# The output projection of a hybrid encoder block as seven half-size products, in two passes over K

## The chip, the cores and the metric

One core of a Trainium2 chip runs the whole block. The metric is device time in microseconds of one execution, as the median of several runs; a profiled execution gives the trace. All matrices are float32. TensorE (PE) is fed float32r: every float32 matrix is split into a high and a low part, and a product is the sum of three matmuls (high x high, high x low, low x high).

## The reference, cut to what matters

```python
h = rmsnorm(x, norm_w)                                  # x: (1, 1024, 2048)
proj = einsum('bsd,de->bse', h, w_in)                   # w_in: (2048, 5632)
q_a, k_a, v_a, g_a, q_r, k_r, v_r, g_r = split(proj)    # 1024,256,256,1024 | 512,512,1024,1024
attn = windowed_attention(q_a, k_a, v_a, sink, rel_bias)          # 16 heads of 64, +-128 tokens
attn = rmsnorm(attn, attn_out_norm_w) * silu(g_a)                 # 1024 wide
ret = bidirectional_retention(rotary(q_r), rotary(k_r), v_r, decays)   # 8 heads, chunks of 128
ret = head_groupnorm(ret, ret_gn_w) * silu(g_r)                   # 1024 wide
mixed = concatenate([attn, ret], axis=-1)                         # (1, 1024, 2048)
x = x + einsum('bse,ed->bsd', mixed, w_out)                       # w_out: (2048, 2048)
return rmsnorm(x, final_norm_w)
```

## The kernel before, in words

The work has three passes of PE, with the smaller engines' work laid beside them.

1. **Input units, first kind** (`STD`, lines 1224 to 1290): six units of 256 columns over the full K of 2048, 16 K-tiles each (keys, values and queries of attention).
2. **Input units, second kind** (`FAST`, 16 units of 256 columns: the gates `ga` and `gr`, the retention's `qk` and `vr`). Each is computed in two halves of K. The first 1024 of K go as **seven products of half size** (Strassen's scheme; `slots`, `prep`, `multiply`, `collect`, lines 1063 to 1168): the weight tiles of a unit are added and subtracted on GpSimd (POOL, `prep_sums`), each of the seven results is split (ACT high part, POOL low part, line 161 under `split`), and multiplied with one of seven sets of four rows `hT`, combined beforehand from the normalised input by `combine`. A product is 4 K-tiles x 3 = 12 matmuls of 128 x 128 by 512 columns. Attention runs beside this pass. The partial results go to DRAM (`yd`). The second 1024 of K go as plain products in a second loop over the 16 units (line 1370 on), which adds `yd` back; retention runs beside it.
3. **Output projection** (line 1427 on): for each half of the tokens and each of four blocks of 512 output columns, 16 K-tiles; the mixed branches are the stationary side, `w_out` the moving side (lines 1456 to 1458). The 112 weight tiles that are streamed are each split by ACT and DVE into rings of three (`w_split`, `w_load`); 16 more are split by ACT and POOL into `hT` for the last column block (lines 1478 to 1480), which runs token block by token block so that each block can be normalised and stored early (`finish_out`, `finish_last`).

Between 2 and 3 lies `mixer` (`mixed_pair`, lines 940 to 977): it loads the gate (`gd`), attention's inverse norm (`rbd`) and the branch output (`md`), multiplies them on POOL, and writes the split result into `hT`. Before it, `gate_post` applies SiLU and stores the gates to `gd`.

**What sets the order.** `point()` is called after every three 512-column matmuls (0.68 us). It lets queues of generators advance: `jobs` (attention, retention; one step every `pace` points), `aux` and `post`, and it sends stores off some points after their data was made. So the program's order is written out by hand; below that, the framework's scheduler may still reorder each engine's instructions by priority when their inputs are expected. `SP` issues nearly all DMAs, in one line; a load that waits for its buffer holds what stands behind it. PSUM has two banks `Ma`, two `Mb`, three `ST`, one `O`. At the third unit of the second loop (u = 2) the kernel drains what is left of attention and its norm, and opens the retention's buffers.

Of the kernel before, what the change touches and what calls it, by code (L numbers as in the profile page):

```python
# [28 lines left out]
FAST = [("ga", 0), ("qk", 0), ("vr", 0), ("gr", 0), ("qk", 1), ("vr", 1), ("gr", 1), ("ga", 1)]  # L29
FAST += [("qk", 2), ("vr", 2), ("gr", 2), ("qk", 3), ("vr", 3), ("gr", 3), ("ga", 2), ("ga", 3)]  # L30

ROWS = [0, 1, 8, 9, 2, 3, 10, 11, 12, 13, 4, 5, 14, 15, 6, 7]
# [6 lines left out]
def hybrid_block(ctx: ExitStack, tc: tile.TileContext, a: dict, out: bass.AP):  # L39
    nc = tc.nc  # L40
    V, A, G, T, SP = nc.vector, nc.scalar, nc.gpsimd, nc.tensor, nc.sync
# [15 lines left out]
    yd = dram.tile([NF, 4, 128, 512], F32, name="yd")  # L57
    rqk = dram.tile([4, 2, 128, S], F32, name="rqk")
# [9 lines left out]


    hT = hp.tile([128, 28, 1024], F32R, name="hT")  # L70
# [10 lines left out]

    cnt = [0]
    phase = [stp]

    def nm(p):
        cnt[0] += 1
        return f"{p}{cnt[0]}"
# [26 lines left out]

    def held(t, bufs):
        tag, n = serial[t.name]

        return t
# [82 lines left out]
    def w_src(i):  # L201
        if i >= W_ALL:
            i -= W_ALL
            return a["w_out"][(16 * (i // 16) + ROWS[i % 16] if i < 64 else i) % 64]
        if i >= W_STD:
            return a["w_half"][i - W_STD]
        u, j = divmod(i, 8)
        return a["w_in"][8 * u + (j + 7) % 8 if u == NS - 1 else i]

    def w_load(i):  # L210
        if i < n_w[0] and i not in wraw and i not in wsp:
            if i < W_STD:
                r = et_("e11")
            elif i < W_ALL:
                r = rt(F32)
            else:
                r = et_(("e11", "e2", "e12", "e2", "e11", "e12", "e2")[(i - W_ALL) % 7])
            SP.dma_start(r, w_src(i))
            wraw[i] = r

    def w_split(i):
        if i < n_w[0] and i not in wsp:
            hi, lo = wpair(i)
            split(hi, lo, wraw.pop(i), G if i < W_ALL else V)
            wsp[i] = (hi, lo)
# [23 lines left out]
    rowq, rdue = deque(), [0]  # L249
    pt, due, pace, adue, apace = [0], [0], [3.0], [0], [2.0]  # L250

    def point():
# [6 lines left out]
        if rowq and pt[0] >= rdue[0]:  # L259
            rdue[0] = max(rdue[0], pt[0] - 1) + 2.4  # L260
            pump(rowq, 1)
# [3 lines left out]

    def rows_in():
        order = list(range(20)) + list(range(24, 28)) + list(range(20, 24))
        lo = None
        for n in range(len(order) + 3):
            if n < len(order):  # L270
                c_load(0, order[n])
            if n >= 3:
                r = order[n - 3]
                first = 16 * (NS - 1) + r // 2 + 3
                if step[0] < first:
                    yield lambda: step[0] >= first
                lo = c_split(r)
                yield
                lo()
                done.add(("row", r))  # L280
            else:
                yield
# [28 lines left out]
    def hx(k, part, c0, c1):  # L311
        if k < 14:
            return hT[:, 2 * k + part, c0:c1]
# [215 lines left out]
    def q_post(i, tiles):  # L529
        for b, t in enumerate(tiles):  # L530
            et, hf = b // 2, b % 2
            for part in range(2):
                x = t2(F32R)
                if part == 0:
                    A.copy(x, t)
                    hi = x
                else:
                    tt(V, x, t, hi.bitcast(F32), ALU.subtract)
                last = (lambda: done.add(("qa", i))) if b == 3 and part else None
                store(qsd[2 * i + et, part, :, 512 * hf : 512 * hf + 512], x.bitcast(F32), x, last, 10)  # L540
            yield
# [163 lines left out]


    fetched = {}

    def ret_job(p):
# [21 lines left out]
        if "vt" not in fetched.get(p, {}):  # L731
            fetch(p, "rk")
            fetch(p, "vt")
            for _ in range(4):
# [48 lines left out]
        def scan(ah, h, q):  # L783
# [15 lines left out]
            if h == 1:  # L799
                gb = cdec[64:128, 8 + 2 * p + ah : 9 + 2 * p + ah]  # L800
                for n in range(5, -1, -1):
                    stt(V, s[64:128, 128 * n : 128 * n + 128], s[64:128, 128 * n + 128 : 128 * n + 256], gb,
                        s[64:128, 128 * n : 128 * n + 128], ALU.mult, ALU.add)
# [24 lines left out]
        def spread(ah, h, on):  # L828
            if True:
# [9 lines left out]
                tt(G, y, v, mhalf[:, :4], ALU.pow)  # L839
                O[ah, h] = (on, mv2, v, y)  # L840

# [18 lines left out]
        def o_tr(ah, h):  # L860
# [14 lines left out]
        for todo in (  # L875
# [40 lines left out]
            for f in held_back:  # L916
                f()
# [10 lines left out]
    omix = {}  # L928

    def orow(kk, hf, part):  # L930
        sl = slice(512 * part, 512 * part + 512)
        if hf == 0:
            n = ROWS.index(kk)
            return hT[:, 16 + n if n < 12 else n - 12, sl]
        return hT[:, 4 + kk, sl] if kk < 12 else omix[kk][part]

    def mixed_pair(pair, hf):

        sl = slice(512 * hf, 512 * hf + 512)
        G_, N_, R_ = {}, {}, {}  # L940

        def loads(kk):
            ring = t2 if kk >= 8 else lambda: rt(F32)
            if kk < 8:
                G_[kk], N_[kk] = ring(), ring()
                SP.dma_start(G_[kk], gd[128 * kk : 128 * kk + 128, sl])
                SP.dma_start(N_[kk], rbd[:, sl])
            R_[kk] = ring()
            SP.dma_start(R_[kk], md[128 * kk : 128 * kk + 128, sl])

        def gates(kk):
            tt(G, G_[kk], G_[kk], N_[kk], ALU.mult)
            tt(G, R_[kk], R_[kk], G_[kk], ALU.mult)

        def high(kk):
            if hf and kk >= 12:
                omix[kk] = (rt(F32R), rt(F32R))
            A.activation(orow(kk, hf, 0), R_[kk], AF.Copy, scale=ew[:, kk : kk + 1])

        def low(kk):  # L960
            stt(V, orow(kk, hf, 1), R_[kk], ew[:, kk : kk + 1], orow(kk, hf, 0).bitcast(F32), ALU.mult, ALU.subtract)
            done.add(("mix", kk, hf))

        plan = []
        for n, kk in enumerate(pair):
            at = 5 * n
            plan.append((at, n, loads, kk))
            if kk < 8:
                at += LAGS[hf][0]
                plan.append((at, n, gates, kk))  # L970
            at += LAGS[hf][1] if kk < 8 else LAGS[hf][0] - 2
            plan.append((at, n, high, kk))
            at += LAGS[hf][2]
            plan.append((at, n, low, kk))
        t0 = pt[0]
        for at, _, f, kk in sorted(plan, key=lambda x: x[:2]):
            yield lambda: pt[0] >= t0 + at
            f(kk)
        yield
# [26 lines left out]
    staged = {}  # L1006

    def c_load(ph, r):
        staged[r] = t2()
        SP.dma_start(staged[r], xd[r] if ph else cd[r])  # L1010

    def c_split(r):
        x = held(staged.pop(r), NT2)
        hi = hT[:, r, 0:512]
        A.copy(hi, x)
        return lambda: tt(V, hT[:, r, 512:1024], x, hi.bitcast(F32), ALU.subtract)

    SP.dma_start(nw, a["nw"])
# [43 lines left out]

    def raw_room(q, which):
        if q < NF:
# [583 lines left out]
```

## Time and profile before

| | us |
|---|---|
| median of 3 runs | 1549.68 (1547.74 to 1553.69) |
| profiled execution, its own time | 1547.16 |
| its span, first to last instruction | 1545.4 |

| stretch of the span | us | what runs |
|---|---|---|
| 0 to 296.0 | 296 | six full units, normalisation of the input |
| 296.0 to 734.0 | 438 | first K half of 16 units, with attention |
| 734.0 to 1177.3 | 443 | second K half of 16 units, with retention |
| 1177.3 to 1535.8 | 358 | output projection |
| 1535.8 to 1545.4 | 10 | after the last matmul |

The profile is read from three sides: how long each engine is busy in a stretch (a busy PE is not PE at its pace, since a matmul's recorded time of 389 ns covers more than the distance to the next one), what an engine waited for, and the order of single instructions.

### The profile page before, as it was taken

To read this page: it belongs to the slowest core of one execution; us is meant where nothing else is said; L and a number is where in the kernel's file an instruction comes from. 1 tells how busy PE (TensorE), PEld (TensorE's weight loads), DVE (VectorE), ACT (ScalarE), POOL (GpSimd) and SP (SyncE) were. 2 spreads that over 40 slices of the span, in tenths; PEclk is the share of its full clock that TensorE was granted. 3 is DMA by queue.
4 is the path that set the end of the run, shared out by engine and by line. 5 is a ranking of instruction groups with operands and counts; after the bars stand their busy time and mean duration, and the time that the engine had idled before them with its cause. 6 is when DMAs were issued, how large, how long until landed. Compare 5 with 4: busy or idle time off the path is not lost.

```text
span 1545.4 us, 21741 instructions
## 1 busy us (share of the span) xinstructions
PE 1503.5 (97%) x7442; PEld 1258.8 (81%) x7442; DVE 787.5 (51%) x1732; ACT 633.2 (41%) x1341; POOL 552.6 (36%) x433
## 2 busy tenths in 40 slices
PE   8999999899999999999999999999999999999997
PEld 6998887777888888887878888788888788887886
DVE  5563335764564664665043735747364433464323
ACT  5311134665775775775212232232324333434210
POOL 3232221347556557546251533525233410113000
PEclk9999999999999999999999999999999999999999
DMA  8889568586456456446566463564636855575403
GB/s 305 294 261 325 187 185 278 183 267 186 135 152 190 126 156 210 149 126 225 174 204 212 163 224 127 181 218 132 232 114 213 277 159 153 179 238 186 124 19 109
DMA packets 185034, 292.83 MB, mean 189 GB/s; under 512 B 28203, under 2 KB 66091, under 8 KB 184284
## 3 DMA queue, kind: packets, MB, share of 16 engines
q1 hardware_dynamic: 152156, 266.28, 53.6%
q10 hardware_dynamic: 32768, 25.17, 5.0%
q8 instruction: 58, 0.95, 0.3%
q14 instruction: 52, 0.43, 0.1%
HBM read 204.84 MB, written 86.54 MB: 189 GB/s over the span
## 4 chain that ended last, share of the span: by engine, by line
PE 76%; DMA 9%; DVE 6%; issue 3%; ACT 3%; POOL 2%; SPq 1%; ACTq 0%; POOLq 0%; DVEq 0%
PE psMa L1403 3%; PE psMb L1403 3%; PE psMa L1405 3%; PE psMa L1404 3%; PE psMb L1404 3%; PE psMb L1405 3%; PE psMa L1100 3%; PE psMa L1101 3%; PE psMa L1102 3%; PE psMb L1100 2%; PE psMb L1102 2%; PE psMb L1101 2%; PE psST L1457 2%; PE psST L1458 2%; PE psST L1456 2%
## 5 line engine op out<-in xcount | busy, mean ns | idle before, releaser
L161 POOL TENSOR_TENSOR wl<-r,wh 128x512 fp32r<-128x512 f32 x176 | 233.0, 1327 | 400.4 <-ACT wh L167 376.0
L167 ACT CAST wh<-e 128x512 fp32r<-128x512 f32 x160 | 97.9, 618 | 213.7 <-PE psMb L1458 63.1
L167 ACT CAST wh<-r 128x512 fp32r<-128x512 f32 x176 | 108.3, 617 | 156.3 <-PE psMb L1404 75.4
L161 DVE TENSOR_TENSOR wl<-e,wh 128x512 fp32r<-128x512 f32 x112 | 88.3, 797 | 133.6 <-ACT wh L167 133.0
L161 POOL TENSOR_TENSOR r<-r,r 128x512 f32<-128x512 f32 x96 | 131.1, 1374 | 53.1 <-DMA r<-rbd 46.3
L161 POOL TENSOR_TENSOR wl<-e,wh 128x512 fp32r<-128x512 f32 x48 | 70.4, 1470 | 198.1 <-ACT wh L167 166.4
L1403 PE MATMUL psMb<-hT,wh 128*128 128x512 f32 x256 | 105.7, 413 | 1.5 <-DVE e L161 1.5
L1100 PE MATMUL psMa<-hT,wh 128*128 128x512 f32 x256 | 102.6, 401 | 2.9 <-DVE e L161 2.9
L1403 PE MATMUL psMa<-hT,wh 128*128 128x512 f32 x256 | 104.0, 406 | 0.3 <-ACT on L853 0.3
L1101 PE MATMUL psMa<-hT,wh 128*128 128x512 f32 x256 | 101.3, 396 | 0.0
L1102 PE MATMUL psMa<-hT,wl 128*128 128x512 f32 x256 | 101.3, 396 | 0.0
L1405 PE MATMUL psMb<-hT,wl 128*128 128x512 f32 x256 | 100.3, 392 | 0.0
L1404 PE MATMUL psMb<-hT,wh 128*128 128x512 f32 x256 | 100.2, 392 | 0.0
L1405 PE MATMUL psMa<-hT,wl 128*128 128x512 f32 x256 | 100.0, 391 | 0.0
L1404 PE MATMUL psMa<-hT,wh 128*128 128x512 f32 x256 | 99.8, 390 | 0.0
L648 DVE CUSTOM_DVE_ANT_0 P<-psST,bias,nsink 128x384 f32<-128x384 f32 (+1 forms) x128 | 74.3, 580 | 33.3 <-PE psST L640 31.8
L652 ACT ACTIVATE P<-P,nmx 128x385 f32<-128x385 f32 (+1 forms) x128 | 75.9, 593 | 34.9 <-DVE nmx L648 33.2
L1100 PE MATMUL psMb<-hT,wh 128*128 128x512 f32 x192 | 75.7, 394 | 0.0
L1102 PE MATMUL psMb<-hT,wl 128*128 128x512 f32 x192 | 75.2, 392 | 0.0
L1101 PE MATMUL psMb<-hT,wh 128*128 128x512 f32 x192 | 75.1, 391 | 0.0
L161 DVE TENSOR_TENSOR PTl<-psST,PTh 128x384 fp32r<-128x384 f32 (+1 forms) x128 | 66.5, 520 | 16.0 <-ACT PTh L629 15.6
L161 POOL TENSOR_TENSOR hT<-t,hT 128x512 fp32r<-128x512 f32 x16 | 21.6, 1351 | 122.1 <-ACT hT L167 122.0
(350 smaller groups left out, 3928.4 us busy)
## 6 DMA issues: line engine op xcount, KB each, us to landing
e<-in_w_out SPq DMA_DIRECT2D x112, 256.0 KB, 3.1
r<-in_w_fast SPq DMA_DIRECT2D x64, 256.0 KB, 3.2
r<-in_w_half SPq DMA_DIRECT2D x64, 256.0 KB, 3.7
e<-yd SPq DMA_DIRECT2D x64, 256.0 KB, 4.0
t<-in_xT SPq DMA_DIRECT2D x31, 512.0 KB, 6.0
e<-in_w_in SPq DMA_DIRECT2D x48, 256.0 KB, 4.8
yd<-e SPq DMA_DIRECT2D x48, 256.0 KB, 3.1
t<-in_x SPq DMA_DIRECT2D x16, 512.0 KB, 5.8
```

Of the source, the lines that this page charges most:

```text
L161: eng.tensor_tensor(o, x, y, op)
L167: A.copy(o_hi, x)
L648: V.tensor_tensor_reduce(x[:, :W], p[:, :W], bias[2 * pr + c][:, k0 : k0 + W], -1.0, nsink[:, head : head + 1], ALU.add, ALU.min, nmx[:, c ...
L652: A.activation(x[:, : W + 1], x[:, : W + 1], AF.Exp, bias=nmx[:, c : c + 1], scale=-1.0, accum_out=sums[:, c : c + 1])
L1100: T.matmul(bank, wh[:, ws], hh, start=(j == 0 and p in (0, 1, 3)), stop=False, skip_group_check=True)
L1101: T.matmul(bank, wh[:, ws], hl, start=False, stop=False, skip_group_check=True)
L1102: T.matmul(bank, wl[:, ws], hh, start=False, stop=(j == 3), skip_group_check=True)
L1403: T.matmul(p, wh[:, ws], hh, start=(w, kk) == (0, 0), stop=False)
L1404: T.matmul(p, wh[:, ws], hl, start=False, stop=False)
L1405: T.matmul(p, wl[:, ws], hh, start=False, stop=last)
L1456: T.matmul(p, mh, wh, start=(k == 0), stop=False)
L1457: T.matmul(p, mh, wl, start=False, stop=False)
```

## The change

What it does, part by part:

- The output projection becomes 16 units. A unit is 256 tokens x 1024 output columns x 1024 of K, done as seven products of 128 x 512 x 512 by the helpers of the input units. Now the mixed branches take the place of the weights (token tiles `xm`, combined on POOL unit by unit), and the combinations of `w_out` take the place of the rows.
- The order is four stages `st = 2 * (half of K) + (half of the columns)` of four units each. Half 0 of K holds attention's first 512 features and retention's first two groups, half 1 the rest. Stages 0 and 1 store partial sums (with x added) to `yo`; stages 2 and 3 add them back and finish.
- The weight combinations (28 rows for each stage) are made once and kept in DRAM (`wc`): `w_copies` copies the 12 that need no arithmetic, DRAM to DRAM, beside attention; `w_combine` makes the other 16 on POOL beside retention, in the free rows 16 to 27. At each stage, rows are loaded from `wc` four at a time as the products free them, and split by ACT and DVE (`rows_tick`).
- `hT` becomes 28 tiles `rows[r]`. Rows are loaded straight into their low half and split there.
- The mixer is gone. Attention's gates are multiplied right after each `ga` unit (`attention_gates`), retention's norm weight is multiplied with its gate, and both are stored to `xm` in the layout that the units load.
- Order of units: `ga` units are spread between the others; the drain of attention moves from u = 2 to u = 4; retention steps come every 3.0 points instead of 2.5.
- `manual_schedule` fixes the order of POOL from the start, and that of PE, DVE, ACT and SP from u = 4, as the program writes it. Some steps return a function that is run one step later, so that an engine isn't reached before its inputs are made.
- The final norm runs per block of 128 tokens as a generator (`finish`), with four scalings on DVE.

```diff
+HALF = [[[0, 1, 2, 3], [8, 9, 10, 11]], [[4, 5, 6, 7], [12, 13, 14, 15]]]
+NO = 16
+    ctx.enter_context(tc.manual_schedule(engines={mybir.EngineType.Pool}))
...
+    def w_copies():
+        plan = []
+        for n in range(48):
+            st, k = divmod(n, 12)
+            p, j = (0, 1, 6)[k // 4], k % 4
+            plan.append((8 * n, SP.dma_start, wc[st, 4 * p + j], w_row(st, p != 0, p == 6, j)))
+        yield from planned(plan)
...
+        for g in range(16):
+            st, j = divmod(g, 4)
+            x = [spare(4 * (g % 3) + n) for n in range(4)]
+            t = 25 * g
+            for n in range(4):
+                plan.append((t + 4 * n, load, st, j, x, n))
+            plan += [
+                (t + 26, less, x, 1, 0), (t + 30, less, x, 3, 1),
+                (t + 34, less_to, x, 3, 0), (t + 38, less_to, x, 2, 3),
+                (t + 35, keep, st, 3, j, x[0]), (t + 39, keep, st, 4, j, x[1]),
+                (t + 43, keep, st, 2, j, x[3]), (t + 47, keep, st, 5, j, x[2]),
+            ]
...
+    def rows_tick():
+        if todo and pt[0] >= max(todo[0][0], rnext[0]):
+            rnext[0] = max(rnext[0], pt[0] - 1) + rgap[0]
+            x = todo.popleft()[1:]
+            row_load(*x)
+            parts.append((pt[0] + 10, row_high, *x))
...
+                if f is row_high:
+                    parts.append((pt[0] + 2, row_low, *x))
...
+        elif q < top[0]:
+            o = q - NF
+            drain(jobs, ("ret", 1 if o < 8 else 3))
+            SP.dma_start(raws[q, x], xm[o // 8, x % 2, 2 * (o % 4) + x // 2])
...
-                kk = ROWS[k] if hf == 0 else k
-                for b in range(4):
-                    p = banks4[b]
-                    mh, ml = mhs[:, 128 * b : 128 * b + 128], mls[:, 128 * b : 128 * b + 128]
-                    T.matmul(p, mh, wh, start=(k == 0), stop=False)
-                    T.matmul(p, mh, wl, start=False, stop=False)
-                    T.matmul(p, ml, wh, start=False, stop=(k == NK - 1))
...
+    def finish(blk, ts):
+        v, y, t = (small(1, x, 2) for x in ("fv", "fy", "ft"))
+        V.tensor_reduce(v, squares[blk], mybir.AxisListType.X, ALU.add)
+        V.tensor_scalar(v, v, 1.0 / D, EPS, ALU.mult, ALU.add)
+        tt(G, y, v, mhalf[:, :1], ALU.pow)
+        yield
+        yield
+        newton(t, v, y)
+        tt(V, y, y, t, ALU.mult)
+        for c in range(4):
+            z = ys[blk][:, 512 * c : 512 * c + 512] if c < 2 else ts[c - 2]
+            stt(V, z, z, y, ys["fw"][:, 512 * c : 512 * c + 512], ALU.mult, ALU.mult)
...
-        if u == 2:
+        if u == 4:
             drain(jobs, ("attn", 3))
...
-            pace[0], apace[0] = 2.5, 2.2
+            pace[0], apace[0] = 3.0, 2.2
+            ctx.enter_context(tc.manual_schedule(engines={e.PE, e.DVE, e.Activation, e.SP}))
...
+        if u == 13:
+            rgap[0] = 3.3
+            for p, at in ((0, 20), (1, 40), (2, 73), (3, 81), (4, 89), (6, 97), (5, 105)):
+                o_rows(pt[0] + at, 0, p)
+        elif u == NF - 1:
+            rgap[0] = 2.0
...
+    for n, (q, p) in enumerate(oslots):
+        o = q - NF
+        st = o // 4
+        prepare(q, p, NF)
+        for x in wanted.pop(n, ()):
+            o_request(*x)
+        rows_done([("row", st, p, j) for j in range(4)])
+        multiply(q, p, between)
+        o_collect(q, p)
+        if o % 4 == 3 and st < 3:
+            rgap[0] = 2.0
+            o_rows(pt[0] + 2, st + 1, p)
```

## Rows read from the trace of the kernel before

**Rows 1.** The page, busy time, share of the span, instructions of an engine.
```profile
PE 1503.5 (97%) x7442; PEld 1258.8 (81%) x7442; DVE 787.5 (51%) x1732; ACT 633.2 (41%) x1341; POOL 552.6 (36%) x433
```
**Rows 2.** Busy time by stretch; last columns: granted clock, DMA share, GB/s.
```profile
1177.30:1535.80 358.50, 354.23 (x1542) 288.92 (x1540) 149.95 (x245) 110.58 (x213) 55.78 (x44) 1.00 0.53 170
734.00:1177.30 443.30, 438.45 (x2238) 365.65 (x2237) 220.44 (x533) 122.27 (x236) 171.01 (x141) 1.00 0.54 177
296.00:734.00 438.00, 426.99 (x2217) 361.70 (x2216) 258.59 (x671) 292.37 (x685) 244.69 (x186) 0.99 0.57 175
6.50:296.00 289.50, 283.86 (x1449) 242.49 (x1450) 153.72 (x274) 103.63 (x200) 78.09 (x53) 0.99 0.77 258
```
**Rows 3.** Timeline of PE in the last column block: start us, us, what.
```profile
1494.80 0.39 PE L1478 MATMUL psMa<-hT 128*128 128x512 f32 x1
...
1495.48 0.39 PE L1478 MATMUL psMa<-hT 128*128 128x512 f32 x1
...
1515.20 0.39 PE L1478 MATMUL psMb<-hT 128*128 128x512 f32 x1
```
**Rows 4.** Busy time by stretch, columns as in rows 2 (PE, PEld, DVE, ACT, POOL).
```profile
1212.00:1219.00 7.00, 5.25 (x16) 3.98 (x16) 6.00 (x5) 2.06 (x4) 6.21 (x4) 0.76 0.63 205
...
296.00:350.00 54.00, 49.07 (x248) 40.37 (x246) 35.27 (x93) 36.04 (x87) 20.69 (x16) 0.97 0.77 237
350.00:734.00 384.00, 377.92 (x1970) 321.33 (x1971) 223.32 (x579) 256.33 (x599) 224.00 (x171) 1.00 0.55 166
```
**Rows 5.** PE's waits, 1177 to 1536 and 734 to 1177 us: total, times, longest.
```profile
PE psMa L1457 <- DVE wl L161: 2.8, 5, 1.5
...
PE psST L187 <- DVE any L161: 2.7, 1, 2.7
PE psMb L1403 <- DVE e L161: 1.5, 1, 1.5
```
**Rows 6.** Timeline of POOL, three places.
```profile
596.88 3.44 POOL L161 TENSOR_TENSOR wl<-r,wh 128x512 fp32r<-128x512 f32 x2
...
613.90 3.92 POOL L161 TENSOR_TENSOR r<-r,r 128x512 f32<-128x512 f32 x3
...
1416.53 1.29 POOL L161 TENSOR_TENSOR hT<-t,hT 128x512 fp32r<-128x512 f32 x1 [1.84 <-ACT hT L167]
```
**Rows 7.** The page's costliest groups: ACT's high parts (count, busy us, mean ns).
```profile
L167 ACT CAST wh<-r 128x512 fp32r<-128x512 f32 x176 | 108.3, 617 | 156.3 <-PE psMb L1404 75.4
```
**Rows 8.** Timeline of DVE at the same places as rows 6.
```profile
596.65 2.52 DVE L161 TENSOR_TENSOR k<-k,k 128x512 fp32r<-128x512 f32 x2 [0.89 <-ACT k L580]
599.09 0.68 DVE L161 TENSOR_TENSOR e<-psMa,e 128x512 f32<-128x512 f32 x1
...
1417.00 1.36 DVE L161 TENSOR_TENSOR wl<-e,wh 128x512 fp32r<-128x512 f32 x1 [3.47 <-ACT wh L167]
...
1424.94 0.69 DVE L161 TENSOR_TENSOR wl<-e,wh 128x512 fp32r<-128x512 f32 x1 [1.34 <-ACT wh L167]
```
**Rows 9.** DMA from 1180 to 1245, then from 740 to 1170 (us to landing last).
```profile
DMA packets 9890, 18.85 MB, mean 290 GB/s; under 512 B 1094, under 2 KB 1094, under 8 KB 9758
...
e<-in_w_out SPq DMA_DIRECT2D x23, 256.0 KB, 4.7
...
vrd<-t ACTq DMA_DIRECT2D x16, 256.0 KB, 3.8
```
**Rows 10.** Timelines of DVE and ACT after the last matmul.
```profile
1535.80 0.76 DVE L1535 TENSOR_TENSOR y<-psMb,t 128x256 f32<-128x256 f32 x2 [4.84 <-PE psMb L1480]
...
1537.25 0.16 DVE L1539 SCALAR_TENSOR_TENSOR fv<-fh,fv 128x1 f32<-128x1 f32 x1 [0.24 <-ACT t L1536]
...
1539.21 1.33 ACT L1546 ACTIVATE y<-y,fy 128x512 f32<-128x512 f32 x2 [2.00 <-DVE fy L1541]
```
**Rows 11.** Groups of DVE by line, 1245 to 1492 us (count, busy us, mean ns).
```profile
L1515 DVE SCALAR_TENSOR_TENSOR y<-y,fy,fw 128x512 f32<-128x512 f32 x16 | 11.3, 748 | 0.1
```
**Rows 12.** SP's waits, 1177 to 1536 us: total, times, longest.
```profile
SPq L218 <- DVE wl L161: 133.9, 85, 4.9
```

More of the change, by code (lines that the diff above doesn't have):

```diff
@@ L264, in point @@
             pump(aux, 1)
[L266 to L282, printed above, removed]
     def drain(queue, until):
@@ L531, in q_post @@
             et, hf = b // 2, b % 2
[L532 to L541, printed above, removed]
+            hi = t2(F32R)
+            A.copy(hi, t)
+            store(qsd[2 * i + et, 0, :, 512 * hf : 512 * hf + 512], hi.bitcast(F32), hi, None, 10)
+            for _ in range(3):
+                yield
+            tt(V, t.bitcast(F32R), t, hi.bitcast(F32), ALU.subtract)
+            last = (lambda: done.add(("qa", i))) if b == 3 else None
+            store(qsd[2 * i + et, 1, :, 512 * hf : 512 * hf + 512], t, t, last, 10)
+            for _ in range(3):
+                yield
     acc = [None]
@@ L733, in ret_job @@
             fetch(p, "vt")
-            for _ in range(4):
+            for _ in range(5):
                 yield
@@ L925, in ret_job @@
         yield
[L928 to L961, printed above, removed]
-            done.add(("mix", kk, hf))
-        plan = []
[L965 to L979, printed above, removed]
@@ L1070, in raw_load @@
             SP.dma_start(raws[q, x], a["w_fast"][q, x])
+        elif q < top[0]:
+            o = q - NF
+            drain(jobs, ("ret", 1 if o < 8 else 3))
+            assert all(("mix", kk, hf) in done for kk in (range(8) if o >= 8 else range(4)) for hf in range(2))
+            SP.dma_start(raws[q, x], xm[o // 8, x % 2, 2 * (o % 4) + x // 2])
     def prep_sums(q, part):
-        if not 0 <= q < NF:
+        if not 0 <= q < top[0]:
             return
@@ L1294, in retention, with prepare @@
         yield from ret_job(p)
-    step[0] = 16 * NS
-    old, coming = deque(), deque()
-    for n, (q, p) in enumerate(slots):
-        slot[0] = n
-        if p == 0 and q:
+    def prepare(q, p, first):
+        if p == 0 and q > first:
             prep_sums(q, 0)
@@ L1316, in hybrid_block @@
             raw_load(q + 1, 1)
+    step[0] = 16 * NS
+    side.append((w_copies(), None))
+    for n, (q, p) in enumerate(slots):
+        slot[0] = n
+        prepare(q, p, 0)
         def between():
@@ new lines, in o_ready, with first_slots @@
+    def o_ready(n):
+        pass
+    def first_slots(w, b):
+        if (w, b) == (1, 0):
+            top[0] = NF + NO
+            raw_room(NF, (2, 0, 3, 1))
+            for x in (0, 2, 3, 1):
+                raw_load(NF, x)
+        elif (w, b) == (3, 0):
+            for x in wanted.pop(-1):
+                o_request(*x)
+            prep(*oslots[0])
+        elif (w, b) == (3, 1):
+            prep_sums(NF, 0)
+            prep_sums(NF, 1)
+        elif (w, b) == (3, 3):
+            prep(*oslots[1])
@@ L1612, in _layout @@
     wo = np.concatenate([wo[:1024][paired(1024)], wo[1024:]])
+    wq = wo.reshape(16, 128, 4, 512)
+    outs = [
+        wq[HALF[half][y], :, 2 * f + z] for half in range(2) for f in range(2) for y in range(2) for z in range(2)
+    ]
     d = {
```

480 lines of the change are left out of this document (253 added, 227 removed).

## The prediction

> **What bounds the kernel now.** I read the page's busy shares first: PE is busy for 97% of the span, no other engine for more than 51% [rows 1]. A busy PE need not be PE at its pace, so I then cut the span at the first and last matmul of each pass: first half of the units with attention 296.0 to 734.0 us, second half with retention to 1177.3, output projection to 1535.8, and 9.6 us after the last matmul [rows 2]. The pace comes from a stretch where nothing disturbs PE: the same line recurs every 0.68 us with two other matmuls between, and from 1494.80 to 1515.20 there are 90 of them, so one 512-column matmul takes 0.2267 us [rows 3]. The output projection has 4 column blocks x 16 K-tiles x 8 token blocks x 3 split terms = 1536 matmuls, 348.2 us at that pace, and lasts 358.5. Only 10.3 us of it is lost, mostly before 1219 us, where the granted clock was 0.76 of full for a while [rows 4], and the longest wait named there is 2.8 us in all [rows 5]. So this pass is bound by its matmul count: taking matmuls out shortens it if the engines that feed PE keep up.
>
> **What the change removes.** Sixteen units of 7 products x 4 K-tiles x 3 terms are 1344 matmuls. 192 fewer x 0.2267 = **-43.5 us**. A unit is then 84 x 0.2267 = 19.04 us, the pass 304.6.
>
> **What must keep up in the new pass.** POOL: each unit needs 7 low parts of token sums and 4 sums of token tiles. Three POOL operations in a row took 3.92 us, 1.31 each [rows 6], so 11 cost 14.4 of the 19.04 us (76%). The same helpers already run in the first pass of the input units, there stretched by attention to 27.4 us a unit (438/16). ACT makes 7 high parts and 7 weight-row casts, 14 x 0.62 = 8.7 us [rows 7]; DVE makes 7 adds from PSUM (0.68) and during a reload 11.6 row low parts (0.69 alone, 1.36 when one meets a POOL operation): 12.8 us, or 20.5 if each of them meets one [rows 8]; what decides between the two is weighed below.
>
> Reloads: the 28 weight rows in SBUF change four times (start and three), four rows per product over about 68 points, 46 us, 2.4 units; that is the 11.6 rows a unit. The trace has one such filling of 28 rows beside units of seven products, at 296 to 350 us: PE was busy 49.07 of 54.0 and the mean clock 0.97, so it lost 4.9 + 1.6 = 6.5 us, with attention starting in it [rows 4]. Bounds per reload: 0 and 6.5. I take half, 3.2, for the three inside the pass: 10 us. It takes the place of the 10.3 us that the old pass lost, **net 0** (bounds -10 and +16, four at 6.5 less 10.3).
>
> DMA: rows loaded inside the pass (92), token tiles (60), x (32), partial results out and back (64), output (32) and some retention leftovers are about 290 transfers of 0.262 MB, 76 MB in 305 us, 250 GB/s; during a reload up to 7.3 MB of rows beside 2.4 units at 3.15 MB, 14.9 MB in 46 us, 324 GB/s. The stretch 6.5 to 296 us moved 258 GB/s with PE busy 283.9 of 289.5 [rows 2]; from 1180 to 1245, at 290 GB/s, 256 KB weight loads landed in 4.7 us [rows 9], and a row has 10 points (6.8 us) from issue to its cast. So I cost it at nothing; were that cover gone, the last rival below is the price. The normalised branches now go out in runs of 512 B; a store of that kind (vrd) landed in 3.8 us [rows 9], nobody waits for it sooner than some 25 points later, cost 0. Filling the rows of the two input passes keeps its 28 and 16 splits and only drops a ring of six buffers on the way: 0, bounds -3 and +3, a wait of the size of the longest two above [rows 5], gone or added where a pass starts.
>
> **What it adds elsewhere.** Beside attention, 48 copies of weight tiles from DRAM to DRAM: 25 MB read and written, 57 GB/s over 438 us, on top of 175 [rows 2]: 232, still under the 258 above. Cost 0, bounds 0 and +5.6 (the idle of that stretch). Beside retention, 64 loads, 64 POOL subtractions and 64 stores make the combined weights, and attention's gates move there (16 POOL and 16 DVE operations, in place of the later mixing, which has 32 POOL, 32 ACT and 32 DVE operations). POOL goes from 171.0 by 84 + 21 to at most 276 of 443 us, 62%; DMA from 177 GB/s by 128 x 0.262 MB / 443 us = 76 to about 253. SP issues all of it; what SP is moved past are stores that wait for data, so late stores now hold loads behind them. PE has no new work there. Its longest waits there were 2.7 and 1.5 us [rows 5], the first at 783 us, where the attention norm was forced at the third unit; it is now forced two units later, 64 points (43 us), and comes by itself. If the clock falls behind such a wait as in the stretch of rows 4 with 0.76, (1 - 0.76) x 7.0 = 1.7, that is -4.4; I take **-3** (bounds -4.4 and +6, a stall of the first pass's size if a fixed order makes PE wait behind a retention step). Work of the last retention group that slides into the output pass only changes place, 0.
>
> The fixed order (POOL throughout, the others from the fifth unit): a waiting instruction now holds everything behind it on its engine. Behind an ACT cast of a late row stand the high parts for PE's slot after next; behind a POOL sum that waits for token tiles stand the low parts. The lookahead is two slots, 5.4 us, less 0.62 and 1.31 for one split: 3.5 us of slack. Within it the order costs 0.
>
> **The tail.** Now 9.6 us from the last matmul: the last add comes in halves and two engines share the scaling [rows 10]. After: add 0.69, then three scalings of the previous block still ahead on DVE (3 x 0.75 [rows 11]), a short chain like the one from 1537.25 to the scaling at 1539.21 (2.0), four scalings of 0.75 on one engine, so the last is done 7.9 us after the last matmul, against 4.7 now (ACT's last scaling ends at 1540.54); with the same 4.9 us behind it, 12.8. **+3** (bounds 0 and +6).
>
> **Sum.** 1545.4 - 43.5 + 0 - 3 + 3 = 1501.9 span; the profiled execution's own time is 1547.2, 1.8 above its span, and 2.5 under the median of the three runs. So 1501.9 + 1.8 + 2.5 = **1506**.
>
> **The port that POOL and DVE share.** The trace: a DVE subtraction with both inputs in SBUF took 0.69 us alone and 1.36 when it began inside a POOL operation, ending 0.54 after it; two POOL and two such DVE operations together took 3.44 us, 1.72 a pair, where POOL alone takes 1.31 [rows 6, 8]. The Trainium skill (SBUF — State Buffer, two separate sides) says that VectorE and GpSimd share a port pair by exclusive lock, and that the loser fully blocks. The trace agrees. By the pair of the trace a reload unit takes 11 x 1.72 + 0.6 x 0.69 = 19.3 us of the pair, against 19.04 of PE: full, but hardly over. By the rule taken as a plain sum, without overlap of ends, it would be the first rival's 22.4.
>
> **Rivals.**
> (1) The pair that POOL and DVE share becomes the bound during reloads: 11 x 1.31 + 11.6 x 0.69 = 22.4 us a unit, 3.4 over PE's, x 2.4 units x 4 reloads = 33, and the final scalings (8 x 0.75 a unit in the last pass) some 3 more. Less the 10 already counted: 1506 + 26 = **1532**. For it: the rows above. Against: they show 1.72 a pair, not 2.0. It turns to a loss only where a reload costs over (1549.7 - 1496) / 4 = 13 us.
> (2) Better: the reloads hide wholly behind the two slots of lookahead, as most of the first pass after 350 us, which lost 384.0 - 377.9 = 6.1 us in 384 [rows 4]. 10 less and the tail's 1 to 2: **1495**.
> (3) Slower: SP's fixed order delays row loads. Held loads land late, ACT waits at the head of its queue, PE's high parts stand behind it. In the old pass SP was held 133.9 us, 85 times, 1.6 each and 4.9 at most, waiting for DVE to free weight buffers [rows 12]. A row that lands in 4.7 us has 2.1 of cover; a hold of 2.8 us on each of 92 rows costs 92 x 0.7 = 64, time 1506 - 10 + 64 = **1560**. It decides against the change from a hold of 2.7 us on. Against it: the rows have buffers of their own that PE frees, not a ring of two or three.
>
> **Chances.** Forecast 0.60, with its own range 1494 to 1520; (1) 0.15; (2) 0.12; (3) 0.13. What a measurement can tell from no change is about 0.5%, 7.7 us. Faster by more: the forecast, (2) and most of (1), 0.85. Within: the rest of (1) and the mild part of (3), 0.05. Slower: 0.10. The range takes in (2) down to 1488 and (1) up to 1538 and leaves out (3) and the edges, some 0.17.
>
> **What would show it.** PE with about 7250 matmuls; the output pass 305 to 320 us long, its idle gathered at three places two or three units long; POOL about 75% busy in it; the wait at 783 us gone; 12 to 13 us behind the last matmul. Rival (1) would show POOL at over 90% in the reloads with PE waiting for POOL's low parts; (3) ACT casts waiting for row loads with landings over 6.8 us. Wrong altogether would be an output pass over 340 us, or a second pass (734 to 1177 us before) longer by 10 us or more with PE waiting for retention's ACT and DVE steps.

## The result, and the profile after

The changed kernel takes 1530.5 us (median of 4 runs, 1526.5 to 1533.1) against 1548.7 (before, now 4 runs): a ratio of 0.988, interval [0.984, 0.993], 18 us faster where 43 were forecast. The direction held, the size did not: 1530.5 lies outside the forecast's own range of 1494 to 1520, and inside the wider one only because that takes in rival (1). The profiled execution spans 1531.3 us, 14.1 less than before; it is the slowest of the four.

The page's first line beside [rows 1]: PE has exactly the 192 matmuls less; DVE and POOL are much busier.

```profile
PE 1463.1 (96%) x7250; PEld 1218.4 (80%) x7250; DVE 922.0 (60%) x1791; ACT 660.4 (43%) x1401; POOL 844.6 (55%) x641
```

Busy time by stretch, to be read beside [rows 2] (PE, PEld, DVE, ACT, POOL, granted clock, DMA share, GB/s). The second pass now ends at 1156.2, the output pass at 1516.7.

```profile
1516.70:1531.30 14.60, 0.04 (x1) 0.00 (x0) 7.58 (x20) 0.72 (x2) 1.10 (x2) 0.67 0.43 144
734.00:1156.20 422.20, 419.30 (x2103) 349.45 (x2102) 239.22 (x460) 111.63 (x217) 260.52 (x204) 1.00 0.78 262
...
1156.20:1516.70 360.50, 334.76 (x1485) 266.15 (x1483) 268.16 (x370) 149.91 (x296) 258.63 (x190) 1.00 0.63 211
```

The account of the 14.1 us. The second pass starts at 734 as before and is 21.1 shorter; 15.5 of that only moved, since 140 retention matmuls (at their own distances) now lie in the output pass; 5.6 is gain. The output pass is 360.5 = 304.7 for its 1344 matmuls (0.2267 us each) + 15.5 + **40.3 lost**, against 10.3 lost before. The tail is 14.6 instead of 9.6. So -43.5 + 30.0 - 5.6 + 5.0 = -14.1: the matmuls went as forecast, and 30.0 us came back in the pass itself.

Where they came back is seen when the pass is cut at the first matmul of each unit. Quiet units take 19.0 us, PE's pace; units 4 and 8, in which most of a new set of weight rows is split, and the last ones do not (units 4, 6, 8, 14 and 15 of 0 to 15):

```profile
1259.40:1284.80 25.40, 21.16 (x86) 15.19 (x85) 24.58 (x23) 13.12 (x26) 20.27 (x14) 1.00 0.81 271
...
1303.80:1322.80 19.00, 19.00 (x85) 15.77 (x84) 4.84 (x7) 4.36 (x7) 13.99 (x12) 1.00 0.56 171
...
1342.20:1366.90 24.70, 20.48 (x85) 15.37 (x84) 23.88 (x23) 15.64 (x30) 22.31 (x15) 1.00 0.79 283
...
1469.50:1493.50 24.00, 20.53 (x86) 15.40 (x86) 20.21 (x33) 7.46 (x17) 16.07 (x14) 1.00 0.69 217
1493.50:1516.70 23.20, 20.01 (x85) 15.32 (x83) 16.14 (x30) 7.04 (x16) 13.28 (x12) 1.00 0.40 139
```

In unit 4, DVE is busy for 24.58 of 25.40 us with 23 operations, and POOL for 20.27 with 14. What an operation takes has changed, as the three timelines of that unit show (POOL, DVE, PE; compare [rows 6, 8]):

```profile
1258.19 3.45 POOL L166 TENSOR_TENSOR wl<-r,wh 128x512 fp32r<-128x512 f32 x2
1261.60 1.74 POOL L166 TENSOR_TENSOR r<-r,r 128x512 f32<-128x512 f32 x1
1263.31 3.44 POOL L166 TENSOR_TENSOR wl<-r,wh 128x512 fp32r<-128x512 f32 x2
```
```profile
1262.11 0.68 DVE L166 TENSOR_TENSOR e<-psMb,e 128x512 f32<-128x512 f32 x1
1262.71 2.89 DVE L166 TENSOR_TENSOR h<-h 128x512 fp32r<-128x512 f32 x2
...
1275.82 2.86 DVE L166 TENSOR_TENSOR h<-h 128x512 fp32r<-128x512 f32 x2
```
```profile
1273.65 0.50 PE L1168 MATMUL psMa<-h,wh 128*128 128x512 f32 x1 [0.73 <-DVE h L166]
1275.35 0.50 PE L1168 MATMUL psMa<-h,wh 128*128 128x512 f32 x1 [0.73 <-DVE h L166]
1277.04 0.50 PE L1168 MATMUL psMa<-h,wh 128*128 128x512 f32 x1 [0.73 <-DVE h L166]
1278.73 0.50 PE L1168 MATMUL psMa<-h,wh 128*128 128x512 f32 x1 [0.73 <-DVE h L166]
```

POOL's operations come every 1.71 us (1258.19 to 1263.31 for three), two of DVE's row low parts (`h<-h`) and an add every 3.41, and PE, which needs one new row for every three matmuls (0.68 us), gets one every 1.70. Only the adds from PSUM keep their 0.68. PE's waits in the pass (us in total, times, longest; before: [rows 5]) name the same two makers, the row low parts and POOL's low parts (3.9 of their 6.6 us in units 14 and 15), and in the last units DVE's adds:

```profile
PE psMa L1168 <- DVE h L166: 7.2, 10, 0.7
PE psMb L1169 <- POOL wl L166: 6.6, 5, 1.6
PE psMa L1167 <- DVE t L166: 3.5, 3, 2.0
PE psO L812 <- DVE ST L169: 3.2, 1, 3.2
...
PE psMb L1168 <- DVE h L166: 2.3, 4, 0.7
```

A wait's name counts only the idle time just before a matmul; a unit's whole loss is read from its length.

The first three units lose 11.2 us. The last 15 rows of the first filling are split there, but the longest single wait is another: in unit 0 PE stands still for 3.2 us, waiting for a retention state (`psO <- ST` above, until 1176.1). In the four microseconds after it the granted clock is 0.61 of full, which costs an estimated (1 - 0.61) x 4 = 1.6 us more. In unit 0 of experiment 3 that wait is 1.1 us and the clock is 1.00 (last line; the first two are the change):

```profile
1156.20:1189.70 33.50, 30.30 (x161) 25.43 (x160) 32.36 (x61) 14.86 (x28) 20.02 (x18) 0.95 0.52 186
...
1176.00:1180.00 4.00, 3.87 (x15) 3.29 (x16) 3.80 (x10) 0.00 (x0) 0.00 (x0) 0.61 0.01 3
...
1160.30:1190.20 29.90, 28.78 (x161) 24.19 (x160) 28.77 (x62) 14.34 (x27) 14.80 (x13) 1.00 0.61 207
```

### The profile page after: what moved, and what is told of

The parts are those of the page before. It is cut to its first block, busy times and chain, and to the rows that moved or that the text cites. A ratio compares the mean times of both kernels' runs of the same rounds, so it can differ in the third digit from the quotient of the medians.

```text
span 1531.3 us, 22172 instructions
## 1 busy us (share of the span) xinstructions
PE 1463.1 (96%) x7250; PEld 1218.4 (80%) x7250; DVE 922.0 (60%) x1791; ACT 660.4 (43%) x1401; POOL 844.6 (55%) x641
## 4 chain that ended last, share of the span: by engine, by line
PE 71%; DMA 9%; DVE 7%; issue 6%; POOL 4%; ACT 2%; SPq 1%; ACTq 0%; DVEq 0%; POOLq 0%
PE psMa L1168 5%; PE psMa L1167 5%; PE psMa L1169 5%; PE psMb L1169 4%; PE psMa L1573 4%; PE psMb L1573 4%; PE psMb L1168 4%; PE psMb L1167 4%; PE psMb L1575 4%; PE psMb L1574 4%; PE psMa L1575 4%; PE psMa L1574 4%; DVE h L166 2%; DMA h<-wc 2%; PE psST L605 2%
## 5 line engine op out<-in xcount | busy, mean ns | idle before, releaser
L166 POOL TENSOR_TENSOR wl<-r,wh 128x512 fp32r<-128x512 f32 x288 | 393.2, 1369 | 400.7 <-ACT wh L172 380.1
L172 ACT CAST wh<-r 128x512 fp32r<-128x512 f32 x288 | 177.5, 619 | 304.2 <-PE psMa L1168 70.8
L1168 PE MATMUL psMa<-h,wh 128*128 128x512 f32 x512 | 201.9, 394 | 7.4 <-DVE h L166 7.2
L1167 PE MATMUL psMa<-h,wh 128*128 128x512 f32 x512 | 203.0, 397 | 4.2 <-DVE t L166 3.5
L1169 PE MATMUL psMa<-h,wl 128*128 128x512 f32 x512 | 200.9, 392 | 0.0
L166 DVE TENSOR_TENSOR h<-h 128x512 fp32r<-128x512 f32 x156 | 174.3, 1146 | 22.9 <-ACT h L1038 22.9
L1169 PE MATMUL psMb<-h,wl 128*128 128x512 f32 x384 | 151.4, 394 | 7.9 <-POOL wl L166 7.8
L1167 PE MATMUL psMb<-h,wh 128*128 128x512 f32 x384 | 151.9, 396 | 3.0 <-ACT e L1201 1.7
L1168 PE MATMUL psMb<-h,wh 128*128 128x512 f32 x384 | 150.8, 393 | 2.4 <-DVE h L166 2.3
L1168 PEld LDWEIGHTS psMa<-h,wh 128*128 128x128 f32 x512 | 96.6, 189 | 29.4 <-DVE h L166 12.8
L1167 PEld LDWEIGHTS psMa<-h,wh 128*128 128x128 f32 x512 | 96.5, 188 | 23.1 <-issue 3.7
L1169 PEld LDWEIGHTS psMa<-h,wl 128*128 128x128 f32 x512 | 96.5, 189 | 21.0 <-POOL wl L166 0.6
L1573 PE MATMUL psMa<-h,wh 128*128 128x512 f32 x256 | 104.0, 406 | 2.5 <-DVE e L166 2.5
L1573 PE MATMUL psMb<-h,wh 128*128 128x512 f32 x256 | 103.4, 404 | 0.0
L1575 PE MATMUL psMa<-h,wl 128*128 128x512 f32 x256 | 100.0, 391 | 0.0
L1038 ACT CAST h<-h 128x512 fp32r<-128x512 f32 x156 | 90.4, 616 | 22.4 <-DMA h<-cd 9.7
L1575 PE MATMUL psMb<-h,wl 128*128 128x512 f32 x256 | 100.0, 390 | 0.0
L1574 PE MATMUL psMa<-h,wh 128*128 128x512 f32 x256 | 99.8, 390 | 0.0
L1574 PE MATMUL psMb<-h,wh 128*128 128x512 f32 x256 | 99.8, 390 | 0.0
```

The source lines that it names most:

```text
L166: eng.tensor_tensor(o, x, y, op)
L172: A.copy(o_hi, x)
L1038: A.copy(rows[r][:, 0:512], rows[r][:, 512:1024].bitcast(F32))
L1167: T.matmul(bank, wh[:, ws], hh, start=(j == 0 and p in (0, 1, 3)), stop=False, skip_group_check=True)
L1168: T.matmul(bank, wh[:, ws], hl, start=False, stop=False, skip_group_check=True)
L1169: T.matmul(bank, wl[:, ws], hh, start=False, stop=(j == 3), skip_group_check=True)
```

## The experiments

Each run was timed in 3 rounds beside the kernel before. The table has the loss against PE's pace by units (length of the unit in the trace, less 84 x 0.2267 us, less the retention matmuls in it). Rows are changed within units 3 to 5, 7 to 9 and 11 to 13; units 12 to 15 finish the output. Losses and tail are read from one profiled execution a run: between runs whose edit does not touch them, the losses of a reload differ by 1 to 2 us (units 3 to 6: 6.6, 5.6 and 5.2 in the change and both runs of experiment 4).

| run | median | ratio to before | units 0-2 | 3-6 | 7-10 | 11-13 | 14-15 | tail |
|---|---|---|---|---|---|---|---|---|
| the change | 1530.5 | 0.988 [0.984, 0.993] | 11.2 | 6.6 | 6.0 | 7.4 | 9.0 | 14.6 |
| row low parts from PSUM | 1514.4 | 0.976 [0.973, 0.979] | 11.5 | 0.1 | 0.7 | 0.1 | 7.5 | 14.6 |
| sums on DVE | 1523.1 | 0.981 [0.978, 0.984] | 6.4 | 3.9 | 4.1 | 8.3 | 4.0 | 14.6 |
| no scaling | 1516.0 | 0.977 [0.974, 0.980] | 10.7 | 5.6 | 6.0 | 6.3 | 0.1 | 5.8 |
| norm weight in PSUM | 1527.5 | 0.985 [0.981, 0.989] | 10.8 | 5.2 | 6.7 | 8.7 | 2.3 | 14.6 |
| less port | 1526.2 | 0.984 [0.981, 0.988] | 7.8 | 6.0 | 9.0 | 8.8 | 1.2 | 13.5 |
| scaling only | 1526.5 | 0.984 [0.981, 0.988] | 12.2 | 5.1 | 6.5 | 8.7 | 1.1 | 12.9 |
| sums and weight | 1519.0 | 0.980 [0.977, 0.983] | 8.9 | 3.9 | 3.9 | 10.1 | 2.2 | 14.6 |
| half the rows by PSUM | 1514.1 | 0.978 [0.975, 0.980] | 9.9 | 0.2 | 2.0 | 0.3 | 8.5 | 14.5 |
| rows and scaling | 1508.9 | 0.975 [0.973, 0.976] | 11.5 | 0.2 | 0.9 | 1.1 | 3.4 | 13.5 |
| all | 1509.6 | 0.975 [0.972, 0.978] | 6.4 | 0.9 | 2.9 | 3.8 | 0.9 | 13.4 |
| the change, scheduler's order | 1587.9 | 1.022 [1.019, 1.025] | | | | | | |
| before, fixed order | 1572.8 | 1.014 [1.010, 1.017] | | | | | | |

**1. Is it the port, late loads, or DVE's own work?**

```diff
+        if key[0] == "row" and key[1] >= 1:
+            if "pz" not in ys:
+                drain(jobs, ("ret", 3))
+                ys["pz"] = pT()
+                V.memset(ys["pz"], 0.0)
+            tt(V, lo, ys["pz"], hi.bitcast(F32), ALU.subtract)
+        else:
+            tt(V, lo, lo.bitcast(F32), hi.bitcast(F32), ALU.subtract)
```


> In the three reloads inside the output pass the row low parts read a PSUM bank of zeros in place of the row's loaded values (the low parts are therefore wrong): the same instruction count and about the same 0.68 us on DVE, but only one input from SBUF. Now the units that hold the reloads lose 6.3, 5.7 and 3.9 + 2.7 us against PE's pace. Theory A (the port pair that DVE and POOL share is full during reloads): these fall to under 1.5 each, POOL's operations there go from 1.6 to 1.3 us, total 1514 to 1520. Theory B (the row loads land late, SP holds them): the losses stay, total 1526 to 1533. Theory C (DVE simply has too much work of its own there): the losses fall by less than half, 1524 to 1530.

`pz` is a PSUM bank of zeros; the retention's last steps are also drained at the first of these rows. The reloads lose 0.1, 0.7 and 0.1 us: theory A, with nothing left over. DVE does as many operations, two of them now in 1.28 us, and POOL's take 1.30 where the change has 1.47 and 1.55 in units 3 to 5. The row loads land as late as in the change (5.2 us from issue in the first two reloads, against 5.3 and 5.2). Unit 4 and the second reload's first two units:

```profile
1260.40:1279.50 19.10, 19.10 (x85) 15.68 (x84) 13.80 (x22) 12.67 (x23) 14.07 (x12) 1.00 0.94 330
...
1317.60:1336.60 19.00, 19.00 (x85) 15.76 (x84) 10.91 (x17) 9.18 (x17) 11.20 (x10) 1.00 1.01 382
1336.60:1356.30 19.70, 19.40 (x85) 15.61 (x84) 13.82 (x22) 15.13 (x30) 16.67 (x14) 1.00 0.98 351
```
```profile
1266.63 1.28 DVE L166 TENSOR_TENSOR h<-psST,h 128x512 fp32r<-128x512 f32 x2
```

At 330 to 382 GB/s PE stands still for nothing in the first two of these units. So neither the rate of the transfers, nor late loads or SP's order, nor the number of DVE's operations made the reloads slow.

**2. What is the fixed order worth?** Both `manual_schedule` lines taken out of the changed kernel, and the same two lines put into the kernel before.

> Both fixed orders taken out, the framework's scheduler orders the engines again. Theory A says that the order is not what costs: the port is as full either way, 1525 to 1540. Theory B (SP's and ACT's fixed order hold loads and casts behind waiting instructions) says that it gets faster, 1505 to 1520.

> The kernel before, with the same two fixed orders (POOL from the start, the others when the retention's buffers open) and nothing else. If the fixed order by itself were a gain, as the scheduler's order costs the changed kernel 57 us, this would be 5 us or more faster than before. I expect the opposite: its program order was written for a scheduler that moves instructions past waiting ones, so PE, ACT and DVE wait behind one another in the mixing and at the start of the output pass, 1555 to 1600.

Without the fixed order the change is a loss, 1588 us; neither range of the first text held. The second pass alone (734 to 1197) takes 41 us more. There it is not the port: POOL is as busy as in the change (260.06 and 260.52 us) and DVE less (230.97 and 239.22). PE waits there for DVE to take results out of PSUM, and the granted clock of the pass falls from 1.00 to 0.97. Before the longest of these waits (6.3 us, until 902.7) DVE stood for 4.96 us, waiting for a step of the retention's norm on POOL, with the add from PSUM behind it. The output pass takes 16 us more; that was not taken apart. The two largest waits of the second pass, DVE before the longest, and the two passes:

```profile
PE psMa L1571 <- DVE e L165: 15.9, 5, 6.3
PE psMb L1571 <- DVE e L165: 8.1, 3, 4.1
```
```profile
897.40 1.22 DVE L165 TENSOR_TENSOR bnt<-bnv,bny 128x4 f32<-128x4 f32 x1 [4.96 <-POOL bny L165]
...
901.89 1.28 DVE L165 TENSOR_TENSOR e<-psMa,e 128x512 f32<-128x512 f32 x2
```
```profile
734.00:1197.40 463.40, 434.20 (x2113) 357.85 (x2112) 230.97 (x464) 114.88 (x219) 260.06 (x208) 0.97 0.73 244
1197.40:1574.30 376.90, 341.81 (x1484) 272.98 (x1484) 252.20 (x369) 150.59 (x296) 251.27 (x185) 0.97 0.59 197
```

The order is no gain by itself either: the kernel before gets 20 us slower with it (1572.8 against 1553.2 in the same rounds), as expected. PE's largest waits are for ACT and POOL; that these are steps which the scheduler moved before is argued, not shown step by step:

```profile
PE psMa L1459 <- ACT wh L168: 8.2, 3, 6.5
PE psMa L1408 <- POOL wl L162: 7.4, 5, 3.7
```

In this kernel a fixed order and a program written for it belong together. The 57 us between the change with and without it are of two sets of rounds; by the ratios to before, it is 52.

**3. Less POOL time in the pair.**

```diff
-        eng = G
+        eng = G if q < NF else V
```


> The four sums of token tiles of each unit of the output pass on DVE (0.69 us alone) in place of POOL (1.31). Theory A: the pair's time in a reload unit falls by 4 x (1.31 - 0.55) = 3 us of a shortage of some 6, so each reload loses about half, total 1520 to 1526. Theory B: DVE now waits for the token tiles as well, no gain or a loss, 1530 to 1540. Theory C: DVE gets 2.8 us a unit more, reloads lose more, 1534 to 1545.

`eng` makes the sums of token tiles; `q < NF` are the input units. 1523.1, within theory A's range: the first two reloads fall from 12.6 to 8.0, the last two units from 9.0 to 4.0; the third reload does not gain (8.3), and of the 4.8 us less at the start, 3.6 are the wait and the clock of unit 0 shown above. In unit 4 DVE now has 26 operations and is busy 21.95 of 22.9 us; 26 x 0.69 = 17.9 of that would be their own time, by an estimate, so DVE is again held in part by POOL:

```profile
1258.40:1281.30 22.90, 20.29 (x86) 15.47 (x86) 21.95 (x26) 12.06 (x22) 10.92 (x8) 1.00 0.87 297
```

**4. The last units.** First the 32 scalings left out (the removed line of the edit, with nothing in its place), then 24 of them reading the norm weight from PSUM, where ACT copies three of its four blocks once.

```diff
+        ys["fp"] = [pS() for _ in range(3)]
...
-            stt(V, z, z, y, ys["fw"][:, 512 * c : 512 * c + 512], ALU.mult, ALU.mult)
+            stt(V, z, z, y, ys["fp"][c] if c < 3 else ys["fw"][:, 1536:2048], ALU.mult, ALU.mult)
```


> The 32 final scalings are left out (the output is not normalised). The last four units lose 15.6 us now and 14.5 us lie behind the last matmul. Theory A: with 8 two-input operations a unit gone, the loss of these units falls by 6 to 9 us and the tail by 4 to 5, total 1517 to 1521; the reloads at the second and third stage (6.3, 5.7) stay. Theory B for this stage (token tiles late because SP is held): the tail falls but the units still lose 11 or more, 1525 to 1528.

> Three of the four blocks of the final norm's weight are copied once into PSUM, so 24 of the 32 final scalings read one input from SBUF instead of two; their number and DVE time stay, and so do the stores that SP holds for them. Theory A (port): the loss of the last four units, 15.6 us, falls by 6 to 8, total 1520 to 1525. Theory B (SP held by stores, token tiles late) and theory C (DVE's own time): the loss stays within 2 us, 1527 to 1532.

Without the scalings units 14 and 15 run at PE's pace (19.2 and 19.1 us), the last four units lose 5.5 instead of 15.6, and the tail is 5.8: theory A, by somewhat more than it said (1516.0).

With the weight in PSUM the verdict is split. The total, 1527.5, lies in the range of theories B and C, not in A's. In the trace the last four units fall from 15.6 to 10.1, of which units 14 and 15 from 9.0 to 2.3, near what A said. The pass of that execution also began 3.7 us later (1159.9; starts vary from 1154.6 to 1160.3 among the runs that keep the fixed order), and units 11 to 13 lost 1.3 more. So the scalings' second input in SBUF causes most of the loss of units 14 and 15: this run changed nothing else but three copies on ACT. It does not tell by which way it does so. Their stores hold SP 15.1 us in these two units instead of 25.7, since the scalings end sooner, and in the change the chain that ended last goes, in unit 14, from a scaling over SP's store to the load of a token tile:

```profile
1482.69 0.67 DVE y L169
...
1483.38 0.34 SPq L1495
...
1483.76 4.78 DMA r<-xm
```

The two units without scalings:

```profile
1469.10:1488.30 19.20, 19.20 (x86) 15.71 (x85) 9.54 (x19) 7.28 (x16) 17.18 (x16) 1.00 0.71 221
1488.30:1507.40 19.10, 19.10 (x85) 15.56 (x83) 7.96 (x22) 6.64 (x15) 10.01 (x10) 1.00 0.64 218
```

**5. Toward a better kernel: three that gained little.** In the first, sums on DVE only in units next to a reload, half of the norm weight multiplied in the third stage, half of the last scalings on ACT; in the second without the sums; the third joins sums on DVE and the weight in PSUM.

> Against the port at three places: sums of token tiles on DVE in the units next to a reload; the norm weight multiplied into the first half of the columns already in the third stage; in the last stage half of the scalings on ACT, the other half on DVE with the weight in PSUM. Theory A: reloads 3 us less each, the last three units 7 to 9 us less, the tail 4 less (two scalings on each of two engines): 1509 to 1516. Theory B: 1522 or more.

> As the run before, without the sums on DVE. Theory A: the reloads lose 6.3 and 5.7 us again, the last units and the tail gain as there: 1516 to 1522. Theory B: 1524 or more.

> The sums of token tiles on DVE and three blocks of the norm weight in PSUM, together. Theory A (port): the two gains of some 7 and 5 us add, 1516 to 1521. If one of them only moved a wait to another place, they don't add: 1523 or more.

The first two missed. In both, the early multiplications put two-input operations into units 8 and 9 (unit 9 loses 1.2 us where it lost none). In the first, the sums of the next unit, made in unit 4, were still POOL's (10 operations there, where experiment 3 had 7), and the reloads stayed at 6.0 and 9.0. The last units gained as expected (units 14 and 15: 1.2 and 1.1 us), but the tail did not: 13.5 and 12.9 against 14.6, where 4 less was expected. By its profiled execution the second is 8.4 us shorter than the change (1522.9 against 1531.3), by the medians only 4.1. The third landed in its range, 1519.0: the gains of the two single runs by their medians, 7.4 and 3.0 us, add up (11.6).

**6. Half the rows by PSUM, with right values.** ACT, which has time, copies every second row's high part to PSUM as well.

```diff
+    hps = {}
...
         A.copy(rows[r][:, 0:512], rows[r][:, 512:1024].bitcast(F32))
+        if key[0] == "row" and key[1] >= 1 and key[3] % 2:
+            drain(jobs, ("ret", 3))
+            hps[key] = pS()
+            A.copy(hps[key], rows[r][:, 0:512].bitcast(F32))
...
-        tt(V, lo, lo.bitcast(F32), hi.bitcast(F32), ALU.subtract)
+        tt(V, lo, lo.bitcast(F32), hps.pop(key) if key in hps else hi.bitcast(F32), ALU.subtract)
```


> In the three inner reloads every second row's high part is also copied to PSUM by ACT (0.62 us more there), and its low part is made from that copy: 14 of 28 DVE operations of a reload read one input from SBUF, all values are right. Theory A: the pair has 7.5 two-input operations less in the worst unit, so the reloads fall from 6.3, 5.7, 6.6 to 1 to 3 each, 1518 to 1524. Theory B (late row loads): no change, 1527 to 1533; ACT's extra work would make it worse.

1514.1, better than expected; the reloads lose 2.5 in all. The timeline of DVE in unit 4 has the matter in six lines: the same subtraction takes 0.67 when one input lies in PSUM, and up to 1.71 when both lie in SBUF. The last line is the unit as a whole:

```profile
1263.13 1.71 DVE L166 TENSOR_TENSOR h<-h 128x512 fp32r<-128x512 f32 x1
1264.77 0.67 DVE L166 TENSOR_TENSOR h<-h,psST 128x512 fp32r<-128x512 f32 x1
1265.36 0.68 DVE L166 TENSOR_TENSOR e<-psMa,e 128x512 f32<-128x512 f32 x1
1265.96 1.65 DVE L166 TENSOR_TENSOR h<-h 128x512 fp32r<-128x512 f32 x1
1267.53 0.68 DVE L166 TENSOR_TENSOR h<-h,psST 128x512 fp32r<-128x512 f32 x1
1268.13 0.68 DVE L166 TENSOR_TENSOR e<-psMb,e 128x512 f32<-128x512 f32 x1
```
```profile
1256.90:1276.20 19.30, 19.30 (x86) 15.71 (x85) 16.99 (x22) 15.99 (x30) 16.54 (x12) 1.00 0.91 323
```

**7. The best.** With the early norm weight and ACT's share of the scalings added, then also the sums on DVE:

> The half rows by PSUM, and the norm weight multiplied into the first half of the columns in the third stage, ACT sharing the scalings of the last stage. Theory A: reloads 1 to 3 us each, last three units under 4 in all, tail 3 to 4 us shorter: 1511 to 1518. Theory B: 1522 or more.

> The same with the sums of token tiles on DVE too. Theory A: POOL then has 7 operations a unit (9.2 us) and the pair has room everywhere, but DVE gets 4 x 0.69 more: if the pair was all, 1506 to 1513; if DVE's own time (26 of 25 us in the worst unit) becomes the bound, no better than the run before or up to 5 us worse.

1508.9 and 1509.6 us, both 0.975 of before, and some 21 us under the change: the two beat both kernels. The first is better than its range, though the tail again fell by 1.1 and not by 3 to 4. The second lies in theory A's range and also fits its second reading (no better than the run before), so it does not tell them apart; it loses less at the start (6.4) but more in the reloads (7.6 against 2.2), in which DVE has the four sums of each unit as well. Between the two there is no difference. The output pass and the tail of the first:

```profile
1155.90:1493.30 337.40, 327.48 (x1485) 266.77 (x1483) 239.53 (x374) 181.65 (x350) 252.94 (x191) 1.00 0.66 224
1493.30:1506.80 13.50, 0.03 (x1) 0.00 (x0) 5.00 (x15) 3.28 (x6) 1.09 (x2) 0.66 0.51 172
```

## Why the prediction was wrong

- **What bounds the kernel, and what the change removes:** right. 7250 matmuls, quiet units at 19.04 us, -43.5.
- **The reloads, "net 0":** this is the step that failed. It says that three reloads cost 3.2 us each, 10 in all, and that these 10 take the place of the 10.3 that the old pass lost. The runs showed 40.3 lost: 20.0 in the reloads, 9.0 in the last two units, 11.2 at the start. So of the 30 us that came back a third lies in the price of a reload, and two thirds in what the step put at nothing.
- **The price of a reload:** 6.6, 6.0 and 7.4 in place of 3.2. The 3.2 was half of what one filling of rows lost in the trace of before, where a unit had 27.4 us and not 19.04. The pair's price was read rightly (1.72; it is 1.70), but the count was an average: 11.6 rows a unit over 2.4 units. The kernel sends a row every two points, 1.36 us, up to 14 in 19.04 us, and 15 of 28 begin in unit 4, the longest, where DVE is busy 24.58 of 25.40 us. That 15 x 1.70 = 25.5 comes so near to 25.4 is in part chance, since POOL made only 14 operations there and paused between some of them. ACT's seven row casts a unit were an average of the same kind, but it was busy for only 13.12 us there. That a two-input pair made the loss is shown (experiments 1 and 6); the exact count is not.
- **What stood at nothing besides:** the last two units (9.0) and the start (11.2). The final scalings are two-input operations too; rival (1) had 3 us for them, the sum none. That the old pass's loss would go had no reason given: it lay mostly at the start of that pass, and the new pass loses at its start again. Of the 11.2, 3.2 is PE's wait for a retention state and 1.6 the lower clock behind it. Where the sums of token tiles are DVE's in every unit, units 0 to 2 lose 6.4, 6.4 and 8.9 (experiment 3, the second of 7 and the third of 5): the wait is 1.1 and 1.3 us with the clock at 1.00 in the two at 6.4, and 3.7 with 0.95 in the other. So it is this wait and the clock that differ. What makes the wait shorter, and the rest of the loss, was not taken apart; experiments 1 and 6 left the rows of the first filling as they were, so a share of the port in it is open.
- **The signs of being wrong:** the prediction called an output pass over 340 us "wrong altogether"; it was 360.5, or 345.0 without the retention matmuls. POOL was busy for 72% of it, near the 75% forecast.
- **Rival (1):** by its mechanism it was this one, 1532 forecast and 1530.5 measured, but that the number is so near is partly luck. It had 33 us for four reloads and 3 for the scalings, where three reloads lost 20.0 and the last two units 9.0; its 2.0 us a pair was too much and its spread over 2.4 units too even. Its sign, POOL at over 90% in the reloads, came only near (20.27 of 25.40 us in unit 4, 22.31 of 24.70 in unit 8), and PE waited for DVE's row low parts more than for POOL's. It had been given 0.15. The runs agree with the rule of the Trainium skill that stood beside it (SBUF — State Buffer, two separate sides), where it is a DVE operation with two SBUF inputs that takes part in the lock: those take turns with POOL's, and those with one input in PSUM do not (experiments 1 and 6). A pair took 1.70 us, though, and not the 2.0 of one whole operation after the other.
- **Rival (3), late loads:** not in the reloads (experiment 1). In the last units SP's held store and a token tile stand in the chain (experiment 4), behind a scaling; how much of the 9.0 us goes that way was not separated.
- **The fixed order at 0:** nothing is gained by undoing it (experiment 2), but the term hid a loss of 52 to 57 us that the order prevents.
- **Second pass, -3:** it was -5.6, and the wait at 783 us is gone. **The copies between DRAM tensors** cost nothing in the end, but not as planned: SP isn't fixed yet there, and the scheduler issued 44 of 48 before 300 us; the pass behind them began 4 us later and had made it up by 734. **POOL in the second pass:** 260.5 of 422 us, 62%, as forecast.
- **The tail, +3:** +5.0. Scalings of both last blocks stand behind each other on DVE, as worked out, but four of the previous block were still ahead and not three. DVE's last scaling ends 9.2 us after the last matmul (1525.9) where 7.9 was worked out, and 5.4 us follow where 4.9 was carried over. DVE's last two scalings:

```profile
1524.51 1.41 DVE L169 SCALAR_TENSOR_TENSOR t<-t,fy,fw 128x512 f32<-128x512 f32 x2
```

## What to carry to other kernels

When POOL is made the steady feeder of PE, count every DVE operation with two SBUF inputs beside it at the price of the pair (here 1.70 us for 128 x 512), and count it in the worst burst, not on average. Moving one of the inputs to PSUM, by an engine that has time, took the operation out of the pair here at no cost to DVE (0.67 us). When a sum lets a new loss take the place of an old one, say why the old one goes. A program order that is fixed must be written for it, and a change that carries its own order can't be judged with the order taken away.

## What the runs showed of the hardware that was not expected

- POOL and DVE alternating on two-input operations of 128 x 512 keep a cycle of 1.70 us with great regularity (PE, POOL and DVE all show it), against 1.31 and 0.67 apart.
- DVE subtractions into float32r take 0.67 to 0.68 us with either input in PSUM and the other in SBUF (`h<-psST,h` and `h<-h,psST`) beside a busy POOL.
- Mostly 256 KB transfers held 375 GB/s over 19.4 us (unit 7 of the change, which lost 0.3 us) and 382 over 19.0 in experiment 1, where PE lost nothing.

```profile
1322.80:1342.20 19.40, 19.38 (x86) 15.70 (x85) 14.28 (x16) 8.84 (x16) 11.61 (x9) 1.00 1.01 375
```
